# Sample attention regrouped into two groups of four sequences, with key pages in half-page tiles

## The chip, the cores and the metric

One core of a Trainium2 chip runs the whole program. The core has a matrix engine (TensorE, PE in the profile, with its weight loads as PEld), a vector engine (DVE), an activation engine (ACT), GpSimd (POOL), a queue engine that issues most transfers (SP), and 16 DMA engines. The metric is the device time of one execution in microseconds (us), from the first to the last instruction and the little that lies around them. About 0.2% (5 us) is what repeated runs of this kernel can tell from no change.

## What is computed

One inference step of a small decoder with two layers, for a prompt of 1024 tokens and for 8 sample sequences of 4 new tokens each, with the same weights. Layer 0 mixes tokens by a gated MLP, layer 1 by sparse attention; a squared-relu MLP follows each. The change lies in layer 1:

```python
q, k, v, qi, ki, wi = dsa_project(h, w_in, pos)       # projections, rotary
sc = index_scores(qi, wi, ki)                          # cheap scores of all keys
_, idx = lax.top_k(sc, 256)                            # per query, the best 256 keys
o = attend(q, k[idx], v[idx])                          # softmax attention over those
return o @ w_out, k, v, ki
```

For the prompt the keys and values are those of the prompt. For a sample sequence they are 1024 past tokens that lie in eight pages of a cache (reached through a page table) and its 4 new tokens. There are 8 query heads of 128 and 2 key/value heads. Nothing is gathered by the top 256: the kernel finds, for each query, the 256th largest score, turns the scores into a mask (0 or a very large negative number) and adds the mask to the attention scores before the softmax.

## The kernel before

The program is traced in program order; a planner then orders the instructions of each engine ahead of the run. It takes ready instructions by their place in the program, may let a later instruction go first when an earlier one is not ready, and keeps the order of any two instructions of which one writes what the other reads or writes (the same region of the same tile). At run time each engine follows its list.

Tokens are cut into nine tiles: 0 to 7 are the prompt (128 tokens each), 8 is the 32 sample tokens. Layer 1 runs in these steps.

**Index scores** (lines 842 to 898). Tile 8 goes first, then 0 to 7. DVE adds up the weighted relu scores of eight heads into `SC[i]` for tiles 2 to 7 (line 895) and into `SCS` for the samples. Tiles 0 and 1 have no more than 256 keys and need no search.

**Threshold searches** (`topk`, line 682, called through `select` and `TOPK_GROUPS`, line 128). Four searches, each over 31 bits from the highest down; one bit counts how many scores are at least the candidate, then corrects the candidate. Group a (the samples) counts on ACT (line 721), group b (tiles 2 and 3) on DVE (line 700), group c (tiles 4 and 5) on ACT, group d (tiles 6 and 7) on DVE. The groups on ACT also count once on DVE before and once after the search. A count is an elementwise compare whose sum is kept (`cnt`); its elementwise output is thrown away into a tile `junk`, of which each group has its own (`junka` to `junkd`). After the bits, lines 732 to 741 turn `SC[i]` into the mask. In program order a is called at tile 8, and b, c, d one after another behind tile 7. `scores(j, ...)` needs the mask of tile j.

**Query projection** (lines 900 to 930), then the **key projection** (`wk`, line 944, nine tiles, 945 to 963): 24 matmuls a tile, a scaling on ACT, the rotary on POOL (`rope_nat`, lines 751 to 756), a transfer out, two transposes and a split into high and low part.

**Sample keys** (`sample_keys`, line 992) for one sequence: two gathers of half its key pages (POOL issues them, 512 KB each, into one of three `raw` tiles), 16 transposes (line 1001), four copies on ACT (line 1002) into a page tile `kt`. The page tiles take the place of the hidden state `H` ("h0" to "h2"), so a page can be written only when the projections that read that part of `H` are done. For each pair of sequences, 32 matmuls of 32 columns (line 1011, four row groups after one another) and eight copies (line 1014) give the scores of one key/value head: `SS[kv]` holds all eight sequences, one tile for each head.

**Value projection** (`value_tile`, line 1018) with sample keys 0 to 5 between its tiles; then `scores(0, kv)` of the prompt with sample keys 6 and 7; then the sample mask is copied to a tile `bs` (line 1043), both `SS` tiles get mask and softmax (lines 1052 and 966 to 968), the value pages are gathered into the same "h0" to "h2" (line 1076), and `sample_values` and `sample_out` finish the samples.

**Prompt attention** (lines 1166 to 1173): `scores(n // 2, n % 2)` for n from 2 to 15, each followed by the `values` of the one before. `scores` puts mask addition and running minimum on DVE (line 1125), `values` transposes, splits (line 204) and multiplies. The output projection and the last MLP follow.

Of the kernel before, what the change touches and what calls it, by code (L numbers as in the profile page):

```python
# [21 lines left out]
P = 128  # L22
# [54 lines left out]
def const_arrays():  # L77
    eye = np.eye(P, dtype=np.float32)
    t = np.arange(P)
    tril = (t[None, :] <= t[:, None]).astype(np.float32)  # L80
    cmask = np.where(t[None, :] <= t[:, None], 0.0, NEG).astype(np.float32)
    r32 = np.arange(32)
    b32, t32 = r32 // 4, r32 % 4
    same = (b32[:, None] == b32[None, :])
    bdm = np.zeros((P, 32), np.float32)
    bdm[:32] = same & (t32[:, None] <= t32[None, :])
    cm4 = np.zeros((P, 4), np.float32)
    cm4[32:64] = np.where(np.arange(4)[None, :] <= t32[:, None], 0.0, NEG)
    r128 = np.arange(P)
    rb, rt = r128 // 16, r128 % 4  # L90
    newm = (rb[:, None] == b32[None, :]).astype(np.float32)
    sel = np.zeros((P, P), np.float32)
    sel[32:64] = (b32[:, None] == rb[None, :]) & (t32[:, None] == rt[None, :])
# [16 lines left out]
    one = np.ascontiguousarray(np.concatenate(  # L110
        [eye, cmask, cm4, newm, sel, wm.reshape(P, 64), q16] + tabs, axis=1))
    one_a = np.ascontiguousarray(np.concatenate([tril, bdm, rep4], axis=1))
    offs, o = {}, 0
    for n, w in (("eye", P), ("cmask", P), ("cm4", 4), ("newm", 32), ("sel", P), ("wm", 64), ("q16", 1),
                 ("cosI", NT * 8), ("sinI", NT * 8), ("cosH", NT * 16), ("sinH", NT * 16)):
# [15 lines left out]
def build(nc, tc, I, O):  # L131
# [549 lines left out]

    def topk(tag, blocks, how, R):
# [10 lines left out]
        junk = tkp.tile([P, max(x.shape[1] for x in blocks)], I8, name="junk" + tag)  # L693
# [250 lines left out]
    wk = quarter(wB, D)  # L944
# [30 lines left out]
    qsz = wslot([P, 2, 4, 2, 2, 4, 4], F32)  # L975
    V.tensor_copy(qsz.rearrange("p v r q a g t -> p (v r q a g t)"), zero.to_broadcast([P, 512]))
    for kv in range(2):
        for pa in range(2):
            src = qs[:, kv * 4:kv * 4 + 4].rearrange("p g (r a t) -> p a r g t", r=4, a=2)[:, pa]
            V.tensor_copy(qsz[:, kv, :, pa, pa], src)  # L980
    SS = [wslot([P, L_S], F32) for _ in range(2)]
    Q4 = L_S // 4
    banks = {}

    def page_bank(bb, w):
        if bb % 3 == 0:
            banks[0] = hp.tile([P, 3 if bb < 6 else 2, w], F32, name="h%d" % (bb // 3))
        return banks[0][:, bb % 3]

    kts = {}  # L990

    def sample_keys(bb):
        kt = kts[bb % 2] = page_bank(bb, 2 * L_S).rearrange("p (v t) -> p v t", v=2)
        for q in range(2):
            kg = raw([P, 1024])
            gather(kg, ck, bb, 1024, idh[q])
            for kv in range(2):
# [4 lines left out]
                S.activation(kt[:, kv, q * 512:(q + 1) * 512], p, AF.Copy)  # L1002
        V.tensor_copy(kt[:, :, PAST:L_S], KTS[:, :, 4 * bb:4 * bb + 4])
        if bb % 2 == 0:
            return
        pr = bb // 2
        for kv in range(2):
            p = ps("px")
            for pa in range(2):
                for j in range(4):  # L1010
                    PE.matmul(p[j * NS:(j + 1) * NS, :Q4], qsz[:, kv, pr, pa].rearrange("p a g t -> p (a g t)"),
                              kts[pa][:, kv, j * Q4:(j + 1) * Q4], start=pa == 0, stop=pa == 1)
            for j in range(4):
                S.activation(SS[kv][pr * NS:(pr + 1) * NS, j * Q4:(j + 1) * Q4], p[j * NS:(j + 1) * NS, :Q4], AF.Copy)

    wk = quarter(wB, D + 256)
# [14 lines left out]
    smp = {}  # L1031

    def sample_mask():
        bs = smp["bs"] = wslot([P, L_S], F32)
        for c0, c1 in CUTS_S:
# [3 lines left out]
            PE.matmul(p[:, :w].rearrange("p (e q) -> p e q", q=P), cst("sel")[SB],  # L1039
                      SCS[:, 0:PAST].rearrange("p (q e) -> p e q", e=8)[:, e0:e1], start=True, stop=True)  # L1040
            if c1 == L_S:
                PE.matmul(p[:, w:w + 4], cst("sel")[SB], SCS[:, PAST:L_S], start=True, stop=True)
            S.activation(bs[:, c0:c1], p[:, :c1 - c0], AF.Copy)

    PN = kvl.tile([NS, 8, 2, 16], F32, name="PN")

    def sample_softmax(kv):
        if kv == 0:
            smp["PT"] = [wslot([P, 4, 8, 2, 16], F32) for _ in range(2)]
        PT = smp["PT"]  # L1050
        mx = bl.tile([P, 2], F32, name="mx", bufs=4)
        V.tensor_tensor_reduce(out=SS[kv], in0=SS[kv], in1=smp["bs"], scale=-ATTN_SCALE, scalar=3.4e38, op0=ALU.add,
                               op1=ALU.min, accum_out=mx[:, 0:1])
        softmax(SS[kv], P, L_S, mx[:, 0:1])
        for q in range(2):
            p = ps()
            for e in range(4):
                o = (4 * q + e) * P
                PE.transpose(p[:, e * P:(e + 1) * P], SS[kv][:, o:o + P], eye)
            S.activation(PT[q][:, :, :, kv], p.rearrange("p (e b r) -> p e b r", e=4, b=8), AF.Copy)  # L1060
        pn = kvl.tile([P, 8, 4], F32, name="pn")
        V.tensor_tensor(pn, SS[kv][:, None, PAST:L_S].to_broadcast([P, 8, 4]),
                        cst("newm").rearrange("p (b t) -> p b t", b=8), op=ALU.mult)
        p = ps()
        PE.transpose(p[:NS, :P], pn.rearrange("p b t -> p (b t)"), eye)
        S.activation(PN[:, :, kv], p[:NS, :P].rearrange("p (b r) -> p b r", b=8), AF.Copy)
# [4 lines left out]
    def fetch_values():  # L1071
        V.tensor_copy(idh[0], idx)
        for bb in range(8):
            vgs.append(page_bank(bb, 2048))
            gather(vgs[bb], cv, bb, 2048, idh[0])

    def sample_values(z):
        PT = smp["PT"]
        p = ps()
        for e in range(9):  # L1080
            for j in range(4):
                lhs = PN[:, 4 * z + j] if e == 8 else PT[e // 4][:, e % 4, 4 * z + j]
                PE.matmul(p[j * NS:(j + 1) * NS, :256], lhs.rearrange("p v r -> p (v r)"),
# [66 lines left out]
    for i in range(NT):  # L1150
        value_tile(i)
        if 2 <= i < 8:
            sample_keys(i - 2)
    probs = []
    for kv in range(2):
        probs.append(scores(0, kv))
        sample_keys(6 + kv)
    sample_mask()
    for kv in range(2):
        sample_softmax(kv)  # L1160
    fetch_values()
# [92 lines left out]
```

## Time and profile before

| | us |
|---|---|
| median of 3 runs | 2440.2 (2437.74 to 2440.53) |
| the profiled execution | 2439.28 |
| its span, first to last instruction | 2436.9 |
| PE busy | 2336.8 (96%) |
| DVE busy | 1692.9 (69%) |
| POOL busy | 1310.4 (54%) |
| ACT busy | 1062.5 (44%) |

The page cuts the span into 40 slices of 61 us and gives each engine's busy share in tenths. Times in the views count from the first instruction. A matmul's duration is modelled to its end and overlaps the next one, so the distance between two starts is what a matmul costs PE.

### The profile page before, as it was taken

The numbers are of one execution on the slowest core, as the hardware profiler recorded it, in microseconds if no ns is written. First come the engines' busy times: TensorE is split into PE (matmuls) and PEld (weight loads), VectorE is DVE, ScalarE is ACT, GpSimd is POOL, SyncE is SP. The second block draws the span as 40 slices with busy tenths as digits, with TensorE's granted clock in tenths as the row PEclk, the third lists the DMA queues.
The fourth block names the chain that finished last, engine by engine and source line by source line (L and its number), as shares of the span: only waits on it lengthen the run. The fifth ranks groups of instructions, "written<-read, shape, count | busy, mean of one in ns | idle before, by whom it ended". The sixth has DMA issues, their size and how long they took to land.

```text
span 2436.9 us, 42780 instructions
## 1 busy us (share of the span) xinstructions
PE 2336.8 (96%) x15961; PEld 2246.2 (92%) x15961; DVE 1692.9 (69%) x3732; ACT 1062.5 (44%) x2164; POOL 1310.4 (54%) x1695
## 2 busy tenths in 40 slices
PE   8999999999999999989988968999999999999998
PEld 7999999999999999988988747899999999999998
DVE  6151257777777777774998879735677777777775
ACT  6232243333333333355865767734333333333335
POOL 2245446676676676561224435414566766766754
PEclk9999999999999999999999979999999999999999
DMA  6211301111111111141223441040111111111111
GB/s 231 61 46 35 123 27 46 47 48 49 44 48 48 49 52 40 55 131 30 84 70 104 142 173 27 10 158 27 44 48 45 48 49 45 51 46 49 53 44 72
DMA packets 180800, 158.38 MB, mean 65 GB/s; under 512 B 10376, under 2 KB 169712, under 8 KB 179568
## 3 DMA queue, kind: packets, MB, share of 16 engines
q1 hardware_dynamic: 176496, 136.78, 18.0%
q0 software_dynamic: 4096, 18.88, 2.3%
q8 instruction: 125, 2.05, 0.4%
q14 instruction: 83, 0.68, 0.1%
HBM read 134.15 MB, written 21.47 MB: 64 GB/s over the span
## 4 chain that ended last, share of the span: by engine, by line
PE 35%; DVE 9%; POOL 4%; issue 4%; ACT 2%; DMA 1%; SPq 0%; another core or an unknown queue 0%; DVEq 0%; POOLq 0%; ACTq 0%
PE ps L242 4%; PE ps L248 4%; PE ps L247 3%; PE px L242 3%; PE px L248 3%; PE px L247 3%; PE ps L590 2%; PE ps L591 1%; PE ps L592 1%; DVE sc L895 1%; POOL st L558 1%; PE pt L1138 1%; PE pt L592 1%; PE pt L591 1%; PE pt L590 1%
## 5 line engine op out<-in xcount | busy, mean ns | idle before, releaser
L581 POOL TENSOR_TENSOR X<-X,scr 128x264 f32<-128x264 f32 x480 | 427.0, 913 | 165.0 <-DVE X L581 119.4
L248 PE MATMUL ps<-h,w 128*128 128x384 f32 (+1 forms) x1344 | 438.3, 326 | 1.6 <-POOL w L204 1.4
L242 PE MATMUL ps<-h,w 128*128 128x384 f32 (+1 forms) x1344 | 437.1, 325 | 0.7 <-DVE scr L909 0.4
L247 PE MATMUL ps<-h,w 128*128 128x384 f32 (+1 forms) x1344 | 435.8, 324 | 0.0
L203 ACT ACTIVATE w<-raw 128x1024 fp32r<-128x1024 f32 (+2 forms) x248 | 250.6, 1012 | 305.6 <-PE px L247 123.3
L204 DVE TENSOR_TENSOR w<-raw,w 128x1024 fp32r<-128x1024 f32 (+1 forms) x211 | 298.4, 1414 | 32.9 <-ACT w L203 32.6
L242 PE MATMUL px<-h,w 128*128 128x384 f32 (+1 forms) x960 | 310.8, 324 | 0.3
L248 PE MATMUL px<-h,w 128*128 128x384 f32 (+1 forms) x960 | 309.8, 323 | 0.0
L247 PE MATMUL px<-h,w 128*128 128x384 f32 (+1 forms) x960 | 309.2, 322 | 0.0
L603 ACT ACTIVATE scr<-ps 128x264 f32<-128x264 f32 x240 | 92.7, 386 | 426.4 <-PE ps L592 380.3
L248 PEld LDWEIGHTS ps<-h,w 128*128 128x128 f32 x1344 | 254.4, 189 | 3.1 <-POOL w L204 1.7
L242 PEld LDWEIGHTS ps<-h,w 128*128 128x128 f32 x1344 | 254.6, 189 | 2.4 <-ACT w L203 1.0
L247 PEld LDWEIGHTS ps<-h,w 128*128 128x128 f32 x1344 | 254.4, 189 | 0.6
L581 DVE TENSOR_TENSOR X<-X,ps 128x264 f32<-128x264 f32 x480 | 197.4, 422 | 64.3 <-PE ps L592 64.3
L581 DVE TENSOR_TENSOR X<-X,px 128x264 f32<-128x264 f32 x480 | 194.2, 422 | 52.2 <-PE px L592 52.2
L581 DVE TENSOR_TENSOR X<-X,pt 128x264 f32<-128x264 f32 x480 | 203.1, 423 | 33.7 <-PE pt L592 29.0
L590 PE MATMUL ps<-A,w 128*128 128x264 f32 x720 | 206.8, 288 | 20.2 <-ACT A L203 20.2
L591 PE MATMUL ps<-A,w 128*128 128x264 f32 x720 | 206.6, 290 | 7.6 <-DVE A L204 7.5
L592 PE MATMUL ps<-A,w 128*128 128x264 f32 x720 | 203.6, 284 | 0.0
L568 POOL TENSOR_TENSOR raw<-raw 128x128 f32<-128x128 f32 x120 | 56.6, 472 | 267.7 <-DMA raw<-in_ffn_w 178.1
L204 DVE TENSOR_TENSOR A<-st,A 128x264 fp32r<-128x264 f32 (+2 forms) x184 | 164.1, 905 | 45.7 <-ACT A L203 45.6
L242 PEld LDWEIGHTS px<-h,w 128*128 128x128 f32 x960 | 180.4, 188 | 1.3 <-DVE X L581 1.2
(397 smaller groups left out, 6326.8 us busy)
## 6 DMA issues: line engine op xcount, KB each, us to landing
raw<-in_ffn_w SPq DMA_DIRECT2D x68, 512.0 KB
raw<-in_ffn_w SPq DMA_DIRECT2D x120, 256.0 KB
X<-xd SPq DMA_DIRECT2D x16, 528.0 KB
raw<-in_a_w_in SPq DMA_DIRECT2D x10, 512.0 KB
GV<-in_x_prompt SPq DMA_DIRECT2D x8, 512.0 KB
raw<-in_a_w_out SPq DMA_DIRECT2D x8, 512.0 KB
raw<-in_b_w_in SPq DMA_DIRECT2D x8, 512.0 KB
raw<-in_b_w_out SPq DMA_DIRECT2D x8, 512.0 KB
```

The source lines that it names most:

```text
L203: S.activation(hi, src, AF.Copy)
L204: (lo_w[0] or V).tensor_tensor(lo, src, f(hi), op=ALU.subtract)
L242: PE.matmul(out, lh, rh, start=first, stop=False)
L247: PE.matmul(out, lh, rl, start=False, stop=False)
L248: PE.matmul(out, ll, rh, start=False, stop=last)
L558: G.tensor_tensor(q[:, 1], q[:, 2], q[:, 1], op=ALU.subtract)
L568: G.tensor_tensor(sm[0], a21, a22, op=ALU.add)
L581: eng.tensor_tensor(x, x, src, op=op)
L590: PE.matmul(p, wh, xh, start=first, stop=False, skip_group_check=not first)
L591: PE.matmul(p, wh, xl, start=False, stop=False, skip_group_check=not first)
L592: PE.matmul(p, wl, xh, start=False, stop=True, skip_group_check=not first)
L603: S.activation(u, p, AF.Copy)
```

## The change

- `SS[z]` now holds four sequences (z = 0 for sequences 0 to 3, 1 for 4 to 7) with both key/value heads, 32 rows a sequence, in place of eight sequences of one head. `newm` and `sel`, constants that pick rows, get a second half.
- `sample_keys` works on one sequence at a time. Each gathered half page is transposed into a tile `kt` of 2 x 512 columns (two buffers in the pool `kvl`), and the matmuls of that half follow at once (`dots`), the two heads of a row group one after the other. Neither the page tiles in `H` nor the copy of the new keys beside the page are there any more.
- Key tiles run in the order 8, 0 to 7, and each is cut in two (`yield`): the transposes and the split of a tile come two tiles later. Sample keys 0 to 2 lie between the key tiles, 3 to 7 between the value tiles, the first softmax too.
- The sample mask is not copied to a tile; the mask addition of a group reads it from the matmul's output in three pieces.
- The value pages are gathered ahead of the second softmax and of `scores(0, ...)`, into "h0" to "h2", which no key page uses now.
- In `topk` the four junk tiles are gone. Two tiles of 1028 bytes a partition stand for them, one written by all counts on DVE, the other by all counts on ACT.

```diff
...
+    junks = [tkp.tile([P, L_S], I8, name="junk%d" % z) for z in range(2)]
+
     def topk(tag, blocks, how, R):
...
-        junk = tkp.tile([P, max(x.shape[1] for x in blocks)], I8, name="junk" + tag)
+        junk_v, junk_a = junks
...
         def count(sc):
             for i, x in enumerate(blocks):
-                V.tensor_scalar(junk[R, :x.shape[1]], x, sc if isinstance(sc, float) else sc[R, i:i + 1], None,
+                V.tensor_scalar(junk_v[R, :x.shape[1]], x, sc if isinstance(sc, float) else sc[R, i:i + 1], None,
                                 op0=ALU.is_ge, op1=ALU.add, accum_out=cnt[R, i:i + 1])
...
-                    S.activation(junk[R, :L], x, AF.Sign, bias=f(cand)[R, i:i + 1], scale=-1.0,
+                    S.activation(junk_a[R, :L], x, AF.Sign, bias=f(cand)[R, i:i + 1], scale=-1.0,
                                  accum_out=cnt[R, i:i + 1])
...
+    def sample_keys(bb):
+        pk = ps("px")
+
+        def dots(j, cols, keys):
+            for kv in range(2):
+                PE.matmul(pk[j * NS:(j + 1) * NS, cols], qsz[:, kv, bb].rearrange("p u g t -> p (u g t)"), keys(kv),
+                          start=kv == 0, stop=kv == 1)
+
+        for q in range(2):
+            kg = raw([P, 1024])
+            gather(kg, ck, bb, 1024, idh[q])
+            kt = kvl.tile([P, 2, 512], F32, name="kt", bufs=2)
+            for kv in range(2):
+                p = ps("ps" if kv else "pt")
+                for e in range(4):
+                    o = e * 256 + kv * HD
+                    PE.transpose(p[:, e * P:(e + 1) * P], kg[:, o:o + HD], eye)
+                S.activation(kt[:, kv], p, AF.Copy)
+            for j in range(2):
+                dots(2 * q + j, slice(0, 256), lambda kv: kt[:, kv, j * 256:(j + 1) * 256])
+        dots(3, slice(256, 260), lambda kv: KTS[:, kv, 4 * bb:4 * bb + 4])
+        rows = slice(bb % 4 * NS, (bb % 4 + 1) * NS)
+        for j in range(4):
+            w = 260 if j == 3 else 256
+            S.activation(SS[bb // 4][rows, j * 256:j * 256 + w], pk[j * NS:(j + 1) * NS, :w], AF.Copy)
+
+    def key_tile(i):
...
         SP.dma_start(ko_s if i == 8 else ko_p[a:b], nat[:n])
+        yield
         p = ps("pt")
...
-            S.activation(bs[:, c0:c1], p[:, :c1 - c0], AF.Copy)
...
+            V.tensor_tensor_reduce(out=SS[z][:, c0:c1], in0=p[:, :c1 - c0], in1=SS[z][:, c0:c1], scale=-ATTN_SCALE,
+                                   scalar=mx[:, i - 1:i] if i else 3.4e38, op0=ALU.add, op1=ALU.min,
+                                   accum_out=mx[:, i:i + 1])
+        softmax(SS[z], P, L_S, mx[:, 2:3])
+        PT[z] = wslot([P, 8, P], F32)
...
-    for i in range(NT):
+    wk = quarter(wB, D)
+    late = []
+    for i in (8, *range(8)):
+        g = key_tile(i)
+        next(g)
+        late.append(g)
+        if len(late) > 2:
+            next(late.pop(0))
+        if i in (3, 5, 7):
+            sample_keys((i - 3) // 2)
+    wk = quarter(wB, D + 256)
+    for g in late:
+        next(g)
+    for i in (8, *range(8)):
         value_tile(i)
-        if 2 <= i < 8:
-            sample_keys(i - 2)
-    probs = []
-    for kv in range(2):
-        probs.append(scores(0, kv))
-        sample_keys(6 + kv)
-    sample_mask()
-    for kv in range(2):
-        sample_softmax(kv)
-    fetch_values()
+        if i in (0, 2, 3, 5, 6):
+            sample_keys({0: 3, 2: 4, 3: 5, 5: 6, 6: 7}[i])
+        if i == 2:
+            sample_softmax(0)
+    for some in ((0, 1, 2), (3, 4, 5), (6, 7)):
+        fetch_values(some)
+    sample_softmax(1)
+    probs = [scores(0, kv) for kv in range(2)]
     for z in range(2):
         sample_values(z)
     H = hidden_state()
```

## Rows read from the trace of the kernel before

**Rows 1.** Page, part 2: busy tenths of TensorE and VectorE in 40 slices.
```profile
PE   8999999999999999989988968999999999999998
...
DVE  6151257777777777774998879735677777777775
```
**Rows 2.** Busy time by stretch: start:end, length, engines' busy us (instructions), TensorE clock, DMA share, GB/s.
```profile
1160.00:1250.00 90.00, 84.89 (x492) 81.77 (x491) 86.16 (x269) 72.40 (x134) 24.49 (x20) 0.95 0.28 84
1250.00:1310.00 60.00, 54.88 (x322) 51.35 (x320) 57.28 (x164) 34.28 (x69) 13.00 (x11) 0.97 0.23 73
1310.00:1400.00 90.00, 79.66 (x597) 67.60 (x598) 67.80 (x205) 60.26 (x141) 48.70 (x94) 0.92 0.45 138
1400.00:1440.00 40.00, 23.91 (x116) 14.05 (x115) 24.38 (x81) 26.63 (x67) 13.69 (x19) 0.64 0.60 218
1440.00:1484.00 44.00, 36.47 (x283) 26.56 (x284) 43.84 (x138) 27.91 (x78) 23.01 (x27) 0.90 0.21 66
1484.00:1607.00 123.00, 120.44 (x682) 102.71 (x681) 93.57 (x253) 81.06 (x155) 48.96 (x49) 0.99 0.06 18
```
**Rows 3.** Junk tiles: line, count, duration ns min/median/max, first and last start.
```profile
L721 ACT ACTIVATE junka<-ssum,sma x31: 1151/1152/1157, 1139.9 to 1246.3; 32x1028 int8<-32x1028 f32 x31
L700 DVE TENSOR_SCALAR_CACHE_REDUCE junka<-ssum,sma x1: 1273/1273/1273, 1254.9 to 1254.9; 32x1028 int8<-32x1028 f32 x1
...
L700 DVE TENSOR_SCALAR_CACHE_REDUCE junkb<-sc,smb x62: 599/673/746, 1178.6 to 1322.7; 128x384 int8<-128x384 f32 x31, 128x512 int8<-128x512 f32 x31
...
L700 DVE TENSOR_SCALAR_CACHE_REDUCE junkb<-sc x2: 546/616/686, 1156.1 to 1174.8; 128x384 int8<-128x384 f32 x1, 128x512 int8<-128x512 f32 x1
...
L721 ACT ACTIVATE junkc<-sc,smc x62: 812/901/997, 1233.1 to 1436.8; 128x640 int8<-128x640 f32 x31, 128x768 int8<-128x768 f32 x31
...
L700 DVE TENSOR_SCALAR_CACHE_REDUCE junkc<-sc,smc x2: 873/940/1006, 1444.5 to 1446.5; 128x640 int8<-128x640 f32 x1, 128x768 int8<-128x768 f32 x1
...
L700 DVE TENSOR_SCALAR_CACHE_REDUCE junkd<-sc,smd x62: 1111/1198/1280, 1301.7 to 1460.9; 128x896 int8<-128x896 f32 x31, 128x1024 int8<-128x1024 f32 x31
```
**Rows 4.** ACT in order of time: search c in a quiet stretch, then a stall.
```profile
1349.25 0.83 ACT L721 ACTIVATE junkc<-sc,smc 128x640 int8<-128x640 f32 x1 [3.21 <-DVE smd L715]
...
1364.20 0.83 ACT L721 ACTIVATE junkc<-sc,smc 128x640 int8<-128x640 f32 x1
...
1422.19 0.63 ACT L203 ACTIVATE t<-raw 128x512 fp32r<-128x512 f32 x1 [10.19 <-issue]
```
**Rows 5.** VectorE in order of time: search d in a quiet stretch, then beside attention work.
```profile
1359.90 1.15 DVE L700 TENSOR_SCALAR_CACHE_REDUCE junkd<-sc,smd 128x896 int8<-128x896 f32 x1
...
1362.82 1.15 DVE L700 TENSOR_SCALAR_CACHE_REDUCE junkd<-sc,smd 128x896 int8<-128x896 f32 x1
...
1448.35 1.13 DVE L700 TENSOR_SCALAR_CACHE_REDUCE junkd<-sc,smd 128x896 int8<-128x896 f32 x1
...
1458.48 1.15 DVE L700 TENSOR_SCALAR_CACHE_REDUCE junkd<-sc,smd 128x896 int8<-128x896 f32 x1
```
**Rows 6.** Attention: mask of tile 6 (POOL), first score of tile 6, last value product (PE).
```profile
1483.25 0.94 POOL L741 TENSOR_SCALAR sc<-sc 128x896 f32<-128x896 f32 x1 [1.03 <-DVE rc L967]
...
1531.51 0.45 PE L242 MATMUL px<-KT,t 128*128 128x448 f32 x1
...
1606.88 0.40 PE L245 MATMUL ps<-raw,VV 128*128 128x512 f32 x1
```
**Rows 7.** Groups of the sample keys, 1310 to 1480: count, busy us, mean ns, idle before.
```profile
L1014 ACT ACTIVATE w<-px 32x257 f32<-32x257 f32 x32 | 12.0, 376 | 1.3 <-PE px L1011 0.8
...
L1002 ACT ACTIVATE h<-pt 128x512 f32<-128x512 f32 x16 | 9.6, 600 | 0.3 <-PE pt L1001 0.2
```
**Rows 8.** PE in order of time: 16 sample products together, then two alone.
```profile
1363.25 1.07 PE L1011 MATMUL px<-h,w 128*32 128x257 f32 x16
...
1366.22 0.62 PE L1011 MATMUL px<-h,w 128*32 128x257 f32 x2
```
**Rows 9.** Waits, 1310 to 1480: who waited for whom, us, times, longest.
```profile
POOL raw L672 <- PE ps L1001: 20.2, 8, 5.4
```

More of the change, by code (lines that the diff above doesn't have):

```diff
@@ L89, in const_arrays @@
     r128 = np.arange(P)
[L90 to L93, printed above, removed]
+    rt = r128 % 4
+    newm = np.zeros((P, 2, 32), np.float32)
+    sel = np.zeros((P, 2, P), np.float32)
+    for z in range(2):
+        rb = 4 * z + r128 // 32
+        newm[:, z] = rb[:, None] == b32[None, :]
+        sel[32:64, z] = (b32[:, None] == rb[None, :]) & (t32[:, None] == rt[None, :])
     wm = np.zeros((P, 2, 32), np.float32)
@@ L110, in const_arrays @@
     one = np.ascontiguousarray(np.concatenate(
[L111 removed]
+        [eye, cmask, cm4, newm.reshape(P, 64), sel.reshape(P, 2 * P), wm.reshape(P, 64), q16] + tabs, axis=1))
     one_a = np.ascontiguousarray(np.concatenate([tril, bdm, rep4], axis=1))
     offs, o = {}, 0
[L114 removed]
+    for n, w in (("eye", P), ("cmask", P), ("cm4", 4), ("newm", 64), ("sel", 2 * P), ("wm", 64), ("q16", 1),
                  ("cosI", NT * 8), ("sinI", NT * 8), ("cosH", NT * 16), ("sinH", NT * 16)):
@@ L943, in build, with softmax @@
     vo_s = O["new_v_sample"][0].rearrange("b t h d -> (b t) (h d)")
-    wk = quarter(wB, D)
-    for i in range(NT):
+    def softmax(sm, n, L, mx):
+        sd, rc = (bl.tile([P, 1], F32, name=x, bufs=4) for x in ("sd", "rc"))
+        S.activation(sm[:n, :L], sm[:n, :L], AF.Exp, bias=mx, scale=-1.0, accum_out=sd[:n])
+        V.reciprocal(rc[:n], sd[:n])
+        G.tensor_scalar(sm[:n, :L], sm[:n, :L], rc[:n], 1.0, op0=ALU.mult, op1=ALU.mult)
+    ck = I["cache_k"][0].rearrange("n (r e) h d -> (n r) (e h d)", e=4)
+    cv = I["cache_v"][0].rearrange("n (r e) h d -> (n r) (e h d)", e=8)
+    qs = scr(256).rearrange("p (h t) -> p h t", h=NK)
+    SP.dma_start(qs, qd[:, :, SEQ:T])
+    qsz = wslot([P, 2, 8, 2, 4, 4], F32)
+    V.tensor_copy(qsz.rearrange("p v b u g t -> p (v b u g t)"), zero.to_broadcast([P, 512]))
+    for kv in range(2):
+        V.tensor_copy(qsz[:, kv, :, kv], qs[:, kv * 4:kv * 4 + 4].rearrange("p g (b t) -> p b g t", b=8))
+    SS = [wslot([P, L_S], F32) for _ in range(2)]
+    def sample_keys(bb):
[8 more added lines that the diff above has]
+            kt = kvl.tile([P, 2, 512], F32, name="kt", bufs=2)
+            for kv in range(2):
+                p = ps("ps" if kv else "pt")
[11 more added lines that the diff above has]
+    def key_tile(i):
         a, b = toks(i)
@@ L963, in build @@
             lo_w[0] = G
-    def softmax(sm, n, L, mx):
-        sd, rc = (bl.tile([P, 1], F32, name=x, bufs=4) for x in ("sd", "rc"))
-        S.activation(sm[:n, :L], sm[:n, :L], AF.Exp, bias=mx, scale=-1.0, accum_out=sd[:n])
-        V.reciprocal(rc[:n], sd[:n])
-        G.tensor_scalar(sm[:n, :L], sm[:n, :L], rc[:n], 1.0, op0=ALU.mult, op1=ALU.mult)
-    ck = I["cache_k"][0].rearrange("n (r e) h d -> (n r) (e h d)", e=4)
-    cv = I["cache_v"][0].rearrange("n (r e) h d -> (n r) (e h d)", e=8)
@@ L973, in build @@
-    qs = scr(256).rearrange("p (h t) -> p h t", h=NK)
-    SP.dma_start(qs, qd[:, :, SEQ:T])
-    qsz = wslot([P, 2, 4, 2, 2, 4, 4], F32)
-    V.tensor_copy(qsz.rearrange("p v r q a g t -> p (v r q a g t)"), zero.to_broadcast([P, 512]))
-    for kv in range(2):
[L978 to L996, printed above, removed]
-            for kv in range(2):
-                p = ps("ps" if kv else "pt")
-                for e in range(4):
-                    o = e * 256 + kv * HD
-                    PE.transpose(p[:, e * P:(e + 1) * P], kg[:, o:o + HD], eye)
[L1002 to L1014, printed above, removed]
@@ L1029, in value_tile, with sample_softmax @@
             lo_w[0] = None
[L1031 to L1035, printed above, removed]
+    PN = kvl.tile([NS, 2, P], F32, name="PN")
+    PT = {}
+    def sample_softmax(z):
+        sel = cst("sel")[SB, z * P:(z + 1) * P]
+        mx = bl.tile([P, 3], F32, name="mxs", bufs=2)
+        for i, (c0, c1) in enumerate(CUTS_S):
             p = ps()
@@ L1038, in sample_mask @@
             w = (e1 - e0) * P
-            PE.matmul(p[:, :w].rearrange("p (e q) -> p e q", q=P), cst("sel")[SB],
+            PE.matmul(p[:, :w].rearrange("p (e q) -> p e q", q=P), sel,
                       SCS[:, 0:PAST].rearrange("p (q e) -> p e q", e=8)[:, e0:e1], start=True, stop=True)
             if c1 == L_S:
-                PE.matmul(p[:, w:w + 4], cst("sel")[SB], SCS[:, PAST:L_S], start=True, stop=True)
-            S.activation(bs[:, c0:c1], p[:, :c1 - c0], AF.Copy)
[L1045 to L1054, printed above, removed]
+                PE.matmul(p[:, w:w + 4], sel, SCS[:, PAST:L_S], start=True, stop=True)
+            V.tensor_tensor_reduce(out=SS[z][:, c0:c1], in0=p[:, :c1 - c0], in1=SS[z][:, c0:c1], scale=-ATTN_SCALE,
[3 more added lines that the diff above has]
+        PT[z] = wslot([P, 8, P], F32)
         for q in range(2):
@@ L1058, in sample_softmax, with fetch_values @@
                 o = (4 * q + e) * P
-                PE.transpose(p[:, e * P:(e + 1) * P], SS[kv][:, o:o + P], eye)
-            S.activation(PT[q][:, :, :, kv], p.rearrange("p (e b r) -> p e b r", e=4, b=8), AF.Copy)
+                PE.transpose(p[:, e * P:(e + 1) * P], SS[z][:, o:o + P], eye)
+            S.activation(PT[z][:, 4 * q:4 * q + 4].rearrange("p e r -> p (e r)"), p, AF.Copy)
         pn = kvl.tile([P, 8, 4], F32, name="pn")
-        V.tensor_tensor(pn, SS[kv][:, None, PAST:L_S].to_broadcast([P, 8, 4]),
-                        cst("newm").rearrange("p (b t) -> p b t", b=8), op=ALU.mult)
+        V.tensor_tensor(pn, SS[z][:, None, PAST:L_S].to_broadcast([P, 8, 4]),
+                        cst("newm")[:, 32 * z:32 * z + 32].rearrange("p (b t) -> p b t", b=8), op=ALU.mult)
         p = ps()
         PE.transpose(p[:NS, :P], pn.rearrange("p b t -> p (b t)"), eye)
-        S.activation(PN[:, :, kv], p[:NS, :P].rearrange("p (b r) -> p b r", b=8), AF.Copy)
+        S.activation(PN[:, z], p[:NS, :P], AF.Copy)
     ON = [scr(256) for _ in range(2)]
     vgs = []
[L1071 to L1074, printed above, removed]
+    def fetch_values(some):
+        if not vgs:
+            V.tensor_copy(idh[0], idx)
+        pages = hp.tile([P, len(some), 2048], F32, name="h%d" % (some[0] // 3))
+        for z, bb in enumerate(some):
+            vgs.append(pages[:, z])
             gather(vgs[bb], cv, bb, 2048, idh[0])
     def sample_values(z):
-        PT = smp["PT"]
         p = ps()
```

8 lines of the change are left out of this document (2 added, 6 removed).

## The prediction

> **What bounds the kernel now.** The busy tenths come first: TensorE is at nine tenths nearly everywhere, and the stretch where it falls lowest is slices 21 to 25 (1218 to 1523 us: 8, 8, 9, 6, 8), where VectorE reads 9, 8, 8, 7, 9, as high as anywhere [rows 1]. That stretch is the one that the change edits. The table of stretches splits it [rows 2]. From 1160 to 1310 VectorE is busy 143.4 of 150 us and TensorE 139.8: index scores and threshold searches share VectorE. From 1310 to 1400, the key and value projections, TensorE works 79.7 of 90 us. From 1400 to 1440 it works 23.9 of 40 at a granted clock of 0.64, so between its levels of 1.2 and 2.4 GHz; DMA is at 0.60 because the value pages arrive, and ACT stands for 10.19 us in front of one query tile that comes in behind them [rows 4]. From 1440 to 1484 VectorE is full (43.84 of 44); from 1484 to 1607 TensorE is (120.4 of 123).
>
> The third view is that of the junk tiles [rows 3], because the searches run through all of this. Search a counts from 1139.9 to 1246.3 on ACT, with its final count on VectorE at 1254.9. Search b counts from 1156.1 on, c from 1233.1 to 1446.5, d from 1301.7 to 1460.9. They overlap: b's first count stands 99 us ahead of a's final one, though the program has it behind, and d runs its 31 bits while c runs its own. The planner was free to do that since each search wrote a junk tile of its own. The mask of tile 6 is ready at 1484.2 (1483.25 + 0.94), and its first score starts at 1531.5 [rows 6], so this chain has 47 us of slack now.
>
> **The change part by part.** Sizes first that have one answer: 160 more constant columns are 82 KB in a load at the start, under transfers that are there anyway, nothing. The mask copy goes (three copies on ACT, some 1.1 us by the 376 ns of [rows 7]); the mask products double to eight, and two long mask additions become six short ones; even.
>
> *Sample keys.* There are 16 gathers, 128 transposes and 32 + 32 copies (12.0 us, and 2 x 9.6 us on ACT [rows 7]) before and after; they move ahead by some 30 to 50 us into the key projection. Products fall from 128 to 64, and 16 small ones for the new keys come. What this removes: the pages no longer wait for `H`, and the value pages no longer wait for the keys, so the hole of 1400 to 1440 (16.1 us of TensorE idle) and part of the 10.3 us of 1310 to 1400 can close [rows 2]. The cutting of key tiles takes the rotary on POOL off TensorE's path there. Against it stands POOL's queue: a gather waits for a free `raw` tile, 20.2 us in eight waits before [rows 9], and behind it on POOL now stand the rotary of the next key tiles and the splits of the value weights; two tiles of distance (24 products each) hide one such wait, whose longest was 5.4 us. The output transfers on SP keep their order. Gain of the part by itself: between 0 (the hole only moves, since 8 MB of value pages still come in one burst in front of the query tiles) and 30 us (26 us of idle and some of the low clock). I take 20.
>
> The order of the new products costs a little. Before, 16 products of four row groups take 1.07 us, 0.067 each; two that stand alone take 0.62, 0.31 each [rows 8]. In the change the two heads of one row group follow each other, so only neighbours of different groups can overlap: 64 products at 0.07 to 0.31 are 4 to 20 us against 8.6 before; I take 12, beside work that has idle time, so 3 on the path. The Trainium skill, TensorEngine Tiling (Array Packing), section Key Properties, says that different tiles of the array work in parallel; the packed rows agree with it, and it speaks against this order, by the 3 us already counted.
>
> *The junk tiles.* This is the small edit that I think decides. All counts on VectorE now write one tile: a's final count, then all of b, then c's first, c's final, then all of d. None of it is read, yet each writes what the one before wrote, so the planner has to keep them in program order. Hence b starts when a's ACT search is over, c when b is over, and d when c's 31 bits on ACT are over. No wait appears at run time (one engine each); the four searches just stand in a row. The rows do not show such an order, so each length is bounded:
>
> - a: 116 us before (1139.9 to 1254.9 + 1.27 [rows 3]). With b off VectorE it ends between 1232 and 1256; I take 1244.
> - b: 31 bits; a bit is two counts (0.67 mean [rows 3]) and two short corrections, 1.6 us, so 51 us alone; 145 us in [rows 3] (1178.6 to 1323.4) with everything beside it. Index scores still share VectorE until 1300. I take 2.8 a bit, 87 us: 1331.
> - c: 3.74 us a bit where ACT is quiet ((1364.20 - 1349.25) / 4, [rows 4]), 116 in all; from 1233.1 to 1436.8 it took 204, 6.6 a bit, with stalls such as the 10.19 us [rows 3, 4]. The copies that move into this stretch (31 us [rows 7]) lie beside it on ACT. Near the lower end, as b and d no longer stand in VectorE's queue before its corrections: 4.6, 143 us, with 4 for the counts before and after: 1478.
> - d: 2.92 us a bit on a quiet VectorE (1362.82 - 1359.90), 5.07 beside attention ((1458.48 - 1448.35) / 2) [rows 5]: 91 to 157. It now falls where attention fills VectorE at 0.76 (93.57 of 123 [rows 2]); once attention has done tiles 0 to 5 it has nothing left but to wait, and d runs at its quiet rate. 3.7 a bit, 115, with 10 for the first count and the mask of tile 6: 1603.
>
> Before, the first score of tile 6 came at 1531.5 and the last value product at 1606.9, 75 us later [rows 6], with products of tile 5 among them. With those done while waiting, I take 62: attention ends at 1665, and what follows needs all of it. A second way agrees: VectorE's work from 1478 on is d (31 x 2.7, two counts of 1.198 mean [rows 3] and the corrections, and 10: 94 us) and the 94 us of the last stretch less some 5 of d's own mask there, 183, which ends at 1661 if VectorE never rests.
>
> So the end moves by 1665 - 1607 = +58 us, and the 17 us that the sample part gains disappear, since TensorE reaches the wait for d sooner and waits longer. On the profiled execution 2439.3 + 58 = 2497; the median of the runs lies 0.9 above it: **2498 us**.
>
> **The rivals.** *Shared tile without order* (0.12). If no order comes of the shared output, b and d still overlap and the sample part alone counts: -17 us, -25 if the burst of value pages finds TensorE busy. VectorE has 22.2 + 15.6 us free between 1310 and 1440 for what comes earlier [rows 2], so up to there it fits: 2415 to 2430. For it: each engine runs its list one after another, no semaphore is needed. Against: the order is made ahead of the run, from what is written. The Trainium skill, PSUM — Partial Sum Buffer, section Engine vs sequencer instructions, calls the queues of ScalarE, VectorE and GpSimd strict FIFO; by that alone the sharing would be free, and this rival's time would come out; the trace's ACT stall agrees with the FIFO.
>
> *The row of searches fits* (0.12). Each at its quiet rate: a to 1232, b at 2.0 to 1294, c at 3.74 to 1414, d at 2.92 to 1515. That is ahead of 1531, tile 6 waits for nothing, and VectorE, free from 1160 on, loses little: 2428 to 2448, even odds of faster and same. It decides at d's end: every us behind 1531 costs up to one. Against: ACT gets 31 us of copies just there.
>
> *ACT stalls under c* (0.10). c at its old 6.6 a bit from 1331 ends at 1540, d at up to 5 a bit at 1690: +120 to +190, 2560 to 2630.
>
> **How the numbers follow.** Forecast, 2460 to 2560: 0.66. The range reaches to the row that fits and a little into the stalls: 2432 to 2570, with about 0.2 outside. About 0.2% (5 us) is what a measurement of this kernel tells from no change. Faster: 0.12 and 0.06; same: 0.06; slower: 0.66 and 0.10.
>
> **What would show it.** After the change, the counts of the two junk tiles: b's first start behind a's final count, d's first behind c's final one, no overlap. VectorE's busy share lower from 1160 to 1300 and full late. TensorE idle, at a lower granted clock, in front of the first 448-column score, which comes near 1600. The hole at 1400 to 1440 gone or smaller, the gathers of cache keys among the key tiles. If b and d overlap, the main step is wrong; if they don't and 448 columns still start near 1531, the bits run faster than I took them; if the gap comes from the gathers, POOL's queue was the wait that I set too low.

## The result and the profile after

The changed kernel takes **2550.4 us** (median of 4 runs, 2544.1 to 2553.6) against 2439.2 in the runs of before beside it: a ratio of 1.045, 95% interval 1.043 to 1.047, so +111 us. The forecast was 2498 (+58), the range 2432 to 2570. The direction and the mechanism came as forecast; the size came out at nearly twice the forecast. The profiled execution took 2550.5, its span 2548.4.

The busy tenths of the page, as in [rows 1], with the granted clock below:

```profile
PE   8999999999999999999888786199999999999998
...
DVE  6241277777777777836873289963777777777775
...
PEclk9999999999999999999989798599999999999999
```

A slice is 64 us here. TensorE falls to one tenth in slice 26, where VectorE reads 9 and the clock 5. The table of stretches answers [rows 2] in its first six lines (start:end, length, busy us of PE, PEld, DVE, ACT and POOL with their instructions, clock, DMA share, GB/s):

```profile
1160.00:1250.00 90.00, 82.00 (x486) 78.08 (x486) 71.59 (x178) 67.29 (x121) 26.84 (x21) 0.98 0.28 82
1250.00:1310.00 60.00, 52.74 (x310) 49.60 (x308) 50.74 (x139) 15.51 (x26) 14.42 (x12) 0.97 0.25 80
1310.00:1400.00 90.00, 72.19 (x495) 56.70 (x495) 38.34 (x131) 47.54 (x109) 40.00 (x84) 0.88 0.39 116
1400.00:1440.00 40.00, 25.92 (x184) 21.05 (x185) 6.72 (x38) 33.50 (x75) 11.92 (x14) 0.80 0.61 223
1440.00:1484.00 44.00, 40.88 (x302) 28.34 (x301) 21.91 (x106) 39.28 (x109) 18.05 (x26) 0.85 0.27 86
1484.00:1607.00 123.00, 78.12 (x401) 59.43 (x399) 119.48 (x319) 58.57 (x126) 34.14 (x41) 0.86 0.06 14
...
1600.00:1620.00 20.00, 0.00 (x0) 0.00 (x0) 19.05 (x41) 0.00 (x0) 0.00 (x0) 0.50 0.00 0
```

VectorE does less than before up to 1484: 189 us against 279, summed over the five stretches. Then it is full (119.5 of 123) while TensorE works 78 of these 123 us, and nothing at all from 1600 to 1620. What VectorE left undone early is the searches, as the junk tiles show (line, count, duration ns, first and last start; it answers [rows 3]):

```profile
L705 DVE TENSOR_SCALAR_CACHE_REDUCE junk<-sc,smb x62: 600/672/748, 1231.3 to 1348.7; 128x384 int8<-128x384 f32 x31, 128x512 int8<-128x512 f32 x31
L726 ACT ACTIVATE junk<-sc,smc x62: 812/888/978, 1354.0 to 1496.3; 128x640 int8<-128x640 f32 x31, 128x768 int8<-128x768 f32 x31
L705 DVE TENSOR_SCALAR_CACHE_REDUCE junk<-sc,smd x62: 1108/1200/1280, 1507.7 to 1637.7; 128x896 int8<-128x896 f32 x31, 128x1024 int8<-128x1024 f32 x31
L726 ACT ACTIVATE junk<-ssum,sma x31: 1151/1152/1153, 1138.8 to 1222.0; 32x1028 int8<-32x1028 f32 x31
...
L705 DVE TENSOR_SCALAR_CACHE_REDUCE junk<-sc,smc x2: 878/946/1014, 1498.3 to 1499.2; 128x640 int8<-128x640 f32 x1, 128x768 int8<-128x768 f32 x1
...
L705 DVE TENSOR_SCALAR_CACHE_REDUCE junk<-ssum,sma x1: 1272/1272/1272, 1225.6 to 1225.6; 32x1028 int8<-32x1028 f32 x1
```

The four searches stand in a row. A's final count ends at 1226.9, b runs behind it until 1349, c behind b until its final count at 1500.2, d behind c until 1639. The counts of no two searches overlap. Who waits for d is seen in order of time on POOL (mask of tile 6) and PE:

```profile
1645.34 0.94 POOL L746 TENSOR_SCALAR sc<-sc 128x896 f32<-128x896 f32 x1 [83.52 <-DVE sc L745]
...
1647.00 0.74 PE L245 MATMUL px<-KT,t 128*128 128x448 f32 x1 [70.37 <-DVE mx L1116]
1647.54 0.57 PE L250 MATMUL px<-KT,t 128*128 128x448 f32 x1
...
1717.67 0.40 PE L245 MATMUL ps<-raw,VV 128*128 128x512 f32 x1
...
1718.31 0.40 PE L248 MATMUL ps<-raw,VV 128*128 128x512 f32 x1
```

The mask of tile 6 is ready at 1646.3 (before 1484.2), TensorE has stood still for 70.4 us when it starts again at 1647.0, and the last value product ends at 1718.7 (before 1607.3 [rows 6]): +111.4 us, the whole difference; what follows takes 829.7 us after and 829.6 before. The release is put down to `mx` of line 1116: the first scores of tile 6 had been multiplied earlier, from 1555 on; VectorE could not add a mask that was not there, so their places in the accumulation memory stayed taken.

### The profile page after: what moved, and what is told of

Same layout as the page of the kernel before. It is cut to its first block, busy times and chain, and to the rows that moved or that the text cites. A ratio compares the mean times of both kernels' runs of the same rounds, so it can differ in the third digit from the quotient of the medians.

```text
span 2548.4 us, 42829 instructions
## 1 busy us (share of the span) xinstructions
PE 2356.4 (92%) x16001; PEld 2250.2 (88%) x16001; DVE 1712.3 (67%) x3730; ACT 1063.9 (42%) x2161; POOL 1310.0 (51%) x1695
## 4 chain that ended last, share of the span: by engine, by line
PE 31%; DVE 10%; POOL 5%; issue 5%; DMA 3%; ACT 3%; SPq 0%; DVEq 0%; POOLq 0%; ACTq 0%
PE ps L245 4%; PE ps L250 3%; PE ps L251 3%; DVE junk L705 3%; PE px L245 3%; PE px L251 3%; PE px L250 3%; PE ps L593 1%; PE ps L594 1%; PE ps L595 1%; POOL st L561 1%; DMA qd<-scr 1%; DMA raw<-in_cache_k,idh 1%; PE pt L595 1%; PE pt L594 1%
## 5 line engine op out<-in xcount | busy, mean ns | idle before, releaser
L584 POOL TENSOR_TENSOR X<-X,scr 128x264 f32<-128x264 f32 x480 | 427.7, 915 | 166.3 <-DVE X L584 119.5
L207 DVE TENSOR_TENSOR w<-raw,w 128x1024 fp32r<-128x1024 f32 (+1 forms) x211 | 296.6, 1406 | 36.5 <-ACT w L206 36.1
```

Source lines behind the costliest of these rows:

```text
L207: (lo_w[0] or V).tensor_tensor(lo, src, f(hi), op=ALU.subtract)
L584: eng.tensor_tensor(x, x, src, op=op)
```

## The experiments

Each starts from one of the two kernels; where it holds several edits, the text names them. Times are medians, ratios go against the runs of before on the same chip.

**The shared junk tiles by themselves.** The kernel before, with the two tiles of the change and nothing else of it:

```diff
+    junks = [tkp.tile([P, L_S], I8, name="junk%d" % z) for z in range(2)]
...
-        junk = tkp.tile([P, max(x.shape[1] for x in blocks)], I8, name="junk" + tag)
+        junk_v, junk_a = junks
...
```

> The kernel before with nothing changed but the junk tiles: one for all counts on VectorE, one for all counts on ACT. Theory (searches in a row): b starts behind a's final count, c behind b, d behind c's final count; TensorE stands empty ahead of tile 6's scores; 2439 + 80 to + 130, so 2520 to 2570. Rival (the sample part costs the 111 us: gathers on POOL, products, pages): within 10 us of 2439.

Measured: 2550.8, ratio 1.046 (1.044 to 1.048). These few lines take all of the loss; the sample part adds or saves nothing beside them. The counts stand in the same row as in the changed kernel: b from 1231.6, c from 1347.8, d from 1512.5 to 1639.1. One stretch of its table:

```profile
1607.00:1640.00 33.00, 0.00 (x0) 0.00 (x0) 31.07 (x71) 0.24 (x1) 0.00 (x0) 0.50 0.00 0
```

TensorE idle, VectorE full, as in the changed kernel. The order is made ahead of the run: no count reads a junk tile.

**Which link costs how much.** The changed kernel, with the VectorE counts of search c (next run: of search a) written into the tile of ACT's counts:

```diff
-                V.tensor_scalar(junk_v[R, :x.shape[1]], x, ...
+                V.tensor_scalar((junk_a if tag == "c" else junk_v)[R, :x.shape[1]], x, ...
```

> The changed kernel with one edit: the two counts that search c makes on VectorE write the tile of the ACT counts. So the row is a, b, d on VectorE, and c follows a alone. If the loss of 112 us lies in d waiting for c's 31 bits (31 of 4.7 us on ACT in the changed kernel): b runs 1231 to 1350 as there, d starts behind it, 31 bits of 2.9 to 5 us, and its mask is ready by 1445 to 1510, ahead of the first 448-column score of 1531; 2446 to 2456. If b's late start behind a is what costs: the time stays above 2480.

> The changed kernel with the other link taken out: the two counts that search a makes on VectorE write the tile of the ACT counts, so b needn't wait for a, and the row is b, c, d. b should run from about 1180 to 1310 as in the kernels with pairs, c 31 bits of 4.7 us to 1455, d from 1460 to 1590 with its first bits at 8 us beside attention. If the row b, c, d is the cause: the loss shrinks by the 40 us that b ends earlier and no more, 2485 to 2515. If the link from a to b is: 2446 to 2456.

The first edit takes c out of the row on both sides: c doesn't wait for b, nor d for c; d still stands behind b.

Measured: 2454.0 with c out of the row (ratio 1.0064, 1.0048 to 1.0079), 2519.2 without the link from a to b (1.0326, 1.0310 to 1.0342). The counts of d, first without c in the row, then without a:

```profile
L705 DVE TENSOR_SCALAR_CACHE_REDUCE junk<-sc,smd x62: 1123/1203/1280, 1357.2 to 1496.2; 128x896 int8<-128x896 f32 x31, 128x1024 int8<-128x1024 f32 x31
```

```profile
L705 DVE TENSOR_SCALAR_CACHE_REDUCE junk<-sc,smd x62: 1122/1198/1280, 1453.2 to 1609.9; 128x896 int8<-128x896 f32 x31, 128x1024 int8<-128x1024 f32 x31
```

Taking c out of the row gives back 96 us; taking away b's wait for a gives back 31, as long as d hangs behind b and c. Together that is more than the 111 that are lost: the two overlap, they don't add. In the second run the mask of tile 6 is ready at 1618.5, 27.8 us earlier than with both links; the time came out 4 us above the expected 2485 to 2515; d's last bits ran to 1611 and not to 1590.

**The sample part without the row of searches.** The changed kernel with tiles shared by searches that hardly overlap: a with c and b with d; then only a with c; and later a with d, b and c with their own (d's first count starts at 1266.1 there and at 1265.7 before, so this sharing holds d up by nothing):

```diff
-        junk_v, junk_a = junks
+        junk_v = junk_a = junks[tag in "bd"]
...
+        junk_v = junk_a = junks["ac" if tag in "ac" else tag]
...
+        junk_v = junk_a = junks["ad" if tag in "ad" else tag]
```

> The changed kernel with the same two junk tiles, but one for groups a and c (both engines) and one for groups b and d. Theory (searches in a row): c runs on ACT beside b and d on VectorE again; d waits only for b, which ended near 1330, so tile 6's mask is ready by about 1510 and nothing waits for it; 2415 to 2445, the 0 to 25 us of the sample part's gain included. Rival (the sample part costs): it stays over 2520.

> As the run with pairs, but three junk tiles: a and c, b, d. Tells what is left of the order b, d: theory: d had slack of 47 us before, so at most 10 us below the run with pairs, 2410 to 2445. If the row b, d still held up the end, 15 us or more below it.

And the control, the kernel before with the same pairs:

> The kernel before with one edit: searches a and c share a junk tile, b and d share the other; nothing of the sample attention changes. With the two pairs the changed kernel took 2448.0, before 2438.1, so 10 us are to be put down to the sample part or to the pairs. Theory 1, it is the sample part: this kernel stays within 0.2% of before (2434 to 2442), since b's last count (1322 before) is out of the way when d needs VectorE. Theory 2, the pairs cost it, because d can start only behind b and a's final count may not pass c's first: 2444 to 2450, with the query projection ending 3 to 5 us later than before's 1304.6, as it did in the kernels with pairs.

> The changed kernel with junk tiles that order nothing that overlaps: a and d share one (a ends at 1255, d starts at 1300), b and c have their own. This is the sample part by itself. The kernel before with the two pairs was 7 us slower than before, the changed one with pairs 10. If the two add: 2440 to 2443, and the sample part costs 2 or 3 us, its gain taken by the key page that waits behind the value pages. If the cost of the pairs is hidden behind that wait: 2446 to 2449.

Measured: 2448.0 with pairs (ratio 1.0037, 1.0023 to 1.0052), 2447.8 with a and c alone (1.0036, 1.0024 to 1.0047), 2446.0 for before with pairs (1.0031, 1.0020 to 1.0043), 2447.1 with a and d (1.0033, 1.0021 to 1.0045). The first two lie 3 us above the 2415 to 2445 that were expected, which counted on a gain of the sample part. Pairs cost before 7 us, the sample part alone costs 9, and together they cost 10 (6 to 13 by the interval), so they don't add in full. In the control, the first of c's ACT counts starts at 1261.8 and not 1233.1 and the last at 1446.3 and not 1436.8, because c's first count has to stand behind a's last. The first mask of c is then 6 us later, and so is the first score of tile 4 (1491.5 and 1485.4); it starts 27 us behind the mask in both, so that it waits for the mask is likely and not shown. In the changed kernel with pairs the first score of tile 4 comes at 1502.7, 60 us behind its mask, and the same delay is hidden.

**Where the sample part's gain went.** The run with a and d sharing, the table of stretches and one row of TensorE:

```profile
1310.00:1400.00 90.00, 70.03 (x505) 56.43 (x503) 64.81 (x183) 54.83 (x127) 40.09 (x84) 0.93 0.39 120
1400.00:1440.00 40.00, 26.93 (x183) 21.36 (x184) 33.60 (x90) 22.83 (x53) 13.27 (x15) 0.80 0.60 224
1440.00:1484.00 44.00, 41.10 (x300) 28.01 (x298) 35.01 (x111) 24.56 (x72) 21.48 (x29) 0.83 0.23 75
1484.00:1607.00 123.00, 122.09 (x701) 103.44 (x699) 97.57 (x281) 89.90 (x181) 53.75 (x59) 1.00 0.08 23
...
1439.18 1.09 PE L982 MATMUL pt<-one,raw 128*128 128x128 f32 x4 [9.60 <-DMA raw<-in_cache_k,idh]
```

From 1310 to 1607 TensorE is busy 260.2 us, before 260.5 [rows 2]. Idle time moved (9.6 us more ahead of 1400, 9.3 less behind) and its sum up to 1607 did not change. But attention ends later in this run, at 1616.5. The whole stretch from the end of the query projection to the end of attention, before and in this run:

```profile
1304.60:1607.30 302.70, 266.17 (x1722) 216.58 (x1721) 234.99 (x693) 198.33 (x443) 135.01 (x187) 0.91 0.28 89
```

```profile
1303.80:1616.50 312.70, 274.06 (x1760) 221.75 (x1759) 239.17 (x688) 198.01 (x441) 128.59 (x186) 0.93 0.27 87
```

It is 10.0 us longer in these two executions: TensorE works 7.9 us more and idles 2.1 more (38.6 against 36.5). The hole of 1400 to 1440 (13.1 us of idle, before 16.1) is still there with another owner, the last half page of keys. POOL's order in the changed kernel says why:

```profile
1415.27 0.95 POOL L675 DMA_INDIRECT h<-in_cache_v,idh  x1 [4.33 <-DVE smc L730]
...
1422.12 0.94 POOL L675 DMA_INDIRECT h<-in_cache_v,idh  x1 [0.31 <-issue]
1423.37 0.93 POOL L675 DMA_INDIRECT raw<-in_cache_k,idh  x1 [0.30 <-issue]
```

Six value gathers of 1 MB go out first, then the key gather, and 16 us after it the transposes start. In program order it stands ahead of them; the planner let them go first (that no `raw` tile was free yet is a likely reason, the trace doesn't show it). An edit that puts them behind all key gathers (the copy of the index that they read is the one that the second key halves use, written after those are issued), on the kernel with pairs:

```diff
-            V.tensor_copy(idh[0], idx)
+            V.tensor_copy(idh[1], idx)
...
-            gather(vgs[bb], cv, bb, 2048, idh[0])
+            gather(vgs[bb], cv, bb, 2048, idh[1])
```

> As the run with pairs, and the value pages are gathered by the index tile that the last key gather reads, so they come behind all key gathers. In the changed kernel the last half key page stood 13.3 us behind six value gathers. Theory: that hole goes, 5 to 13 us below the run with pairs. Rival: the value pages then hold up the sample products or the query tile by as much, within 3 us.

Measured: 2439.3, ratio 1.0005 (0.9994 to 1.0016): 8.7 us back, about the length of the wait (9.8 in the run with pairs, 0.7 here), and the same time as before within the measurement. The last key gather is issued at 1416.2, the first value gather at 1421.6.

**TensorE's own work.** The groups of the sample products, first before, then the run with a and d sharing (count, busy us, mean ns):

```profile
L1011 PE MATMUL px<-h,w 128*32 128x257 f32 x128 | 19.0, 451 | 0.0
...
L1039 PE MATMUL ps<-ssum,one 32*128 32x384 f32 (+1 forms) x6 | 4.3, 829 | 0.0
```

```profile
L971 PE MATMUL px<-kt,w 128*32 128x256 f32 x128 | 21.7, 418 | 9.4 <-DVE w L963 6.0 <-ACT kt L983 3.3
...
L1037 PE MATMUL ps<-ssum,one 32*128 32x384 f32 (+1 forms) x12 | 8.1, 804 | 0.0
L971 PE MATMUL px<-KTS,w 128*32 128x4 f32 x32 | 2.2, 175 | 0.0
```

Two records stand for one float32 product of the code. The half-page products are as many as before (128 records) and take 2.7 us more, those for the new keys 2.2, the mask products 3.8. To see which of it lies on the path, on the kernel with pairs and values last: the products of a half page head by head, so that the two row groups follow each other; the mask products on the upper halves of the same words, as bfloat16; and both.

```diff
-            for j in range(2):
-                dots(2 * q + j, slice(0, 256), lambda kv: kt[:, kv, j * 256:(j + 1) * 256])
+            dots((2 * q, 2 * q + 1), slice(0, 256), lambda kv, j: kt[:, kv, j % 2 * 256:(j % 2 + 1) * 256])
...
+    def high(x):
+        return x.bitcast(BF16).rearrange("p (n t) -> p n t", t=2)[:, :, 1]
```

> Pairs, value gathers behind the key gathers (2439.3 so far), and the products of a half page in the other order: for one head both row groups, then the other head. In the run without this edit the 128 recorded products of whole columns took 18.1 us from start to start, 0.141 each; two of different row groups that follow each other start 0.007 apart and then 0.21 passes, 0.11 each. If the order counts on the path: 14 us in place of 18, so 2435 to 2437. If the planner had put them side by side already, or the stage has idle time that takes it up: 2438 to 2441.

> Pairs, values last (2439.3 so far), and the products that spread the sample mask over the 128 rows read the upper 16 bits of the mask and of the selecting rows as bfloat16 (both hold only 0, 1 and a power of two, so nothing is lost). Before the change 8 such products took 4.26 us from start to start, 0.53 each; the change has 16, 8.45 us. If this term, which the prediction called even, is on TensorE's path, most of it comes back: 16 at 0.15 or less, 2.4 us, 6 us gained, 2432 to 2435. If the idle time around the value pages takes it up: 2438 to 2441.

> Pairs, values last, products with heads outermost, and mask products in bfloat16, the three together: the candidate for a version ahead of before. If both terms lie on TensorE's path, their gains add: 2428 to 2432. If only one does: 2432 to 2436. If the stage is bound by transfers and not by TensorE's work: 2437 to 2441, like before.

Measured: 2436.3 (ratio 0.9989, 0.9981 to 0.9998) for the order; 2438.1 (0.9997, 0.9988 to 1.0006) for bfloat16; 2435.3 (0.9988, 0.9979 to 0.9997) for both. The groups, order and then bfloat16:

```profile
L972 PE MATMUL px<-kt,w 128*32 128x256 f32 x128 | 16.8, 388 | 1.1 <-DVE w L963 0.7 <-ACT kt L984 0.4
```

```profile
L1040 PE MATMUL ps<-ssum,one 32*128 32x384 bf16 (+1 forms) x6 | 4.5, 771 | 0.0
```

The order takes 3.5 us off TensorE (20.3 without it) and the ratio falls by 0.16%, 4 us; the two intervals together leave some 0.5 to 7, so that all of it counts agrees with the measurement and isn't shown by it. The mask products lose half their records and 4.1 us of busy time (8.6 without the edit), and less than the measurement can tell comes of it; what took that up isn't shown.

**All three on one kernel**, with the junk tiles of the run with a and d:

> The kernel with value gathers behind the key gathers, heads outermost and bfloat16 mask products (2435.3 with pairs), and the junk tiles of the run beside it: a and d share one, b and c have their own. If c's late start in the pairs (its first count had to stand behind a's last) is still on the path, the 7 us come back: 2427 to 2431, the fastest so far. If c's end is no longer what attention waits for: 2433 to 2437.

Measured: 2435.8, ratio 0.9987 (0.9978 to 0.9996). The freer junk tiles give nothing on top of the pairs, which agrees with c's end no longer being what attention waits for. This and the one before it are the fastest versions, 0.12 to 0.13% below before, less than the 0.2% that one tells from no change for certain.

## Why the prediction was right, and where its size failed

**Right.** *The junk edit decides, through the order of the planner.* B, c and d each start behind the one before, and the edit alone makes the loss. The rival of a shared tile without order is refuted: with strict order on each engine it should have been free. The Trainium skill, PSUM — Partial Sum Buffer, section Engine vs sequencer instructions, has those queues as strict FIFO; no run here speaks against that, but the FIFO's contents are fixed ahead of the run, and there the shared output costs 113 us (2438.1 to 2550.8). *The sample part disappears in the wait:* the changed kernel and the edit alone take 2550.4 and 2550.8. *Signs:* VectorE emptier early and full late, TensorE idle at a lower clock in front of tile 6, no time lost behind attention: all there. The hole of 1400 to 1440 hardly got smaller (14.1 us of idle, before 16.1), and 1310 to 1400 lost more (17.8, before 10.3). The "first 448-column score near 1600" was a badly chosen sign: the first products of tile 6 ran at 1555, and the wait came in the middle of them; the moment at which the mask of tile 6 is ready is the one to read.

**The sum, term by term.** The end of attention was put at 1665 and came at 1718.7; the 53.7 us missing are four terms:

| | taken | measured | missing |
|---|---|---|---|
| b's end (a's end 1244, measured 1226.9) | 1331 | 1350.5 | 20 |
| c with its counts | 147 | 149.7 | 3 |
| d, to the mask of tile 6 | 125 | 146.1 | 21 |
| from there to the last value product | 62 | 72.4 | 10 |

*B* is the term that missed most: from a's end to its own it took 124 us where 87 were taken, and 17 of the 37 are hidden in the table by luck, since a ended that much earlier than assumed, below its lower bound of 1232. 2.8 us a bit were taken, it ran at 3.8 (1231.3 to 1350.5, over 31), although VectorE was busy only 122 of 150 us from 1160 to 1310. Its first four bits, beside the last index scores, took 6.3 to 10.5 us each, from one 384-column count to the next; a bit's four instructions each stand behind whatever the planner put between them. Before, b ran still slower, at 4.7 a bit [rows 3], but early.

*D*: 3.7 us a bit were taken, it ran at 4.25, and its first counts and the mask took 14 us where 10 were taken. The bound beside attention, 5.07 a bit [rows 5], came from two bits; the first four of d took 8.6 to 10.7. The 896-column counts of two bits in a row, first beside attention and then in the quiet:

```profile
1528.53 1.14 DVE L705 TENSOR_SCALAR_CACHE_REDUCE junk<-sc,smd 128x896 int8<-128x896 f32 x1
...
1537.16 1.13 DVE L705 TENSOR_SCALAR_CACHE_REDUCE junk<-sc,smd 128x896 int8<-128x896 f32 x1
...
1595.76 1.15 DVE L705 TENSOR_SCALAR_CACHE_REDUCE junk<-sc,smd 128x896 int8<-128x896 f32 x1
...
1598.67 1.15 DVE L705 TENSOR_SCALAR_CACHE_REDUCE junk<-sc,smd 128x896 int8<-128x896 f32 x1
```

The quiet rate, 2.91, was right to a hundredth (2.92). The loaded one was not a bound: how much attention work stands between two bits is for the planner to choose, and two bits of another stretch bound nothing.

*C*: 4.6 a bit was right by two errors. The lower bound of 3.74, read in a stretch where ACT was quiet [rows 4], was no bound, since d's counts on VectorE (1.15 and 1.28 us a bit) stood in front of c's corrections there, and ACT had the copies of the sample keys between c's counts. With d out of the way the changed kernel has bits of 2.46:

```profile
1429.27 0.83 ACT L726 ACTIVATE junk<-sc,smc 128x640 int8<-128x640 f32 x1 [0.48 <-DVE smc L730]
...
1431.73 0.83 ACT L726 ACTIVATE junk<-sc,smc 128x640 int8<-128x640 f32 x1 [0.48 <-DVE smc L730]
```

Longer bits made up for it, beside the projections first (5 to 6 us, one of 14.3), beside attention later (three of 8.5 to 8.6).

*The tail*: 62 assumed that all of tile 5 was done in the wait; that held, but tiles 6 and 7 took 72, of the 75 that they and tile 5's rest took before. Where the 10 us went the rows don't split; the lower clock behind the wait is some 2 of them, an estimate from a dozen products that start 0.37 us apart in place of 0.20.

**The second way of adding up** (VectorE's work of 94 + 89 us from 1478, ending at 1661) failed on both sides. The table of stretches goes on behind 1607 with:

```profile
1607.00:1720.00 113.00, 70.07 (x355) 56.36 (x356) 84.34 (x195) 41.79 (x73) 23.71 (x21) 0.79 0.04 12
```

VectorE worked 119.5 + 84.3 = 204 us from 1484 to 1720 and rested for 32. Counted as the sum was, from c's end (1500.2) to the end of attention, it worked 189 us, 6 more than summed, and rested for 29, most of them behind d, where it waits mainly for ACT's half of the splits (line 206). So of the 58 us by which 1661 was too early, c's later end makes 22, the rest that was put at nothing 29, and the work only 6.

**Wrong: the sample part by itself.** A gain of 17 was taken (bounds 0 to 30, less 3); it costs 8.7. Three steps failed. First, "the hole only moves" was named as the end at 0, but that the value gathers could go in front of a key gather was not: the section looked at what a gather waits for on POOL, not at what overtakes it there. Putting it right gave 8.7 back. Second, "products fall from 128 to 64" compared records of the trace with products of the code (the 32 matmuls for a pair of sequences are records too, the code has 16); they do not fall, and 32 records come on top. Third, "even" for the mask counted copies on ACT against products on TensorE, 3.8 us on the engine that bounds the kernel, though the bfloat16 run shows little of it in the time. What stays open is why closing the hole gave no gain beyond that: in the profiled execution with the values last TensorE is idle 31 us between the end of the query projection and the end of attention, 5 less than before, and does 5 us more work, and the stretch is as long as before (302.5 and 302.7). That the added products are the cause fits with this; a run speaks for it only in the 4 us of their order, and the rest is argued. That kernel also shares its junk tiles in pairs, which cost 7 us in the kernel before.

## What to carry to other kernels

A scratch output that nobody reads is still an output: where a planner or compiler keeps the order of writes, give every independent chain its own, or share only between chains that do not overlap in the trace (a and d here). When a change makes chains follow each other, take a chain's rate from what the engine will have beside it there, not from a quiet or busy stretch elsewhere, and leave wide room upward. When large transfers are freed to start early, look at which small urgent one they can now overtake.

## What the runs showed of the hardware that was not expected

After the 70 us without a matmul the clock was granted at 0.50, 1.2 GHz, and TensorE came back at that level: the 448-column products of 1647.5 to 1648.7 start 0.37 to 0.38 us apart, those of 1652.5 to 1653.3 0.20 to 0.21 (granted 1.00). After a wait of 1.3 us it was back at 0.50 from 1655 to 1658, with starts of such products 0.37 us apart again (1657.0 to 1658.2), and from 1658.2 on they are 0.20 to 0.21 apart where one follows another directly. A key gather of 512 KB that was issued 1.25 us behind the last of six 1 MB gathers kept TensorE waiting 13.3 us in the changed kernel; issued ahead of them, 0.7. And 16 float32 records of the mask products became 8 in bfloat16 with hardly another modelled duration for each of the long ones (804 to 814 ns in float32, 771 in bfloat16).
